# A hybrid attention and delta-rule layer on one core: blocks of the transposed probabilities moved inside SBUF, two more units for the heads, another slab order

## Chip, core and metric

One core of a Trainium2 chip runs one layer in float32. The metric is the time of one execution in microseconds on the device (us); before and after are compared by the medians of several runs. The profile is of one execution of its own, taken by the hardware profiler.

## What is computed

x is 512 x 1024. After an RMS norm, one wide projection gives the inputs of two branches, and of their gates:

```python
q = apply_rope(rms_norm(heads(aq, 8, 128), q_norm), cos, sin)      # attention: 8 heads
k = apply_rope(rms_norm(heads(ak, 2, 128), k_norm), cos, sin)      # 2 kv heads
v = heads(av, 2, 128)
s = einsum('qd,sd->qs', q_i, k) * 128 ** -0.5                      # per head, 512 x 512
o_att = softmax(s) @ v
y_att = (o_att * silu(az)) @ w_br_att
o_dn = bidir_gated_deltanet(...)                                   # delta rule, both directions
y_dn = (rms_norm(o_dn) * silu(dz)) @ w_br_dn
mix = (sigmoid(gate_att) * y_att + sigmoid(gate_dn) * y_dn) @ w_out
x = x + rms_norm(mix, norm_post)
x = x + rms_norm(sigmoid(x @ w_ple_gate) * (p @ w_ple_proj), ple_norm)
```

The change concerns the step from softmax(s) to its product with v, and the order in which the projections' weights come.

## The kernel before

**Matmuls.** A float32 product is made of three matmuls on halves that add up to the operand: lo x hi, hi x lo and hi x hi. `split` (L250) makes them: a cast on ACT gives hi, and a subtraction on DVE or on POOL gives lo, whichever the planner holds to be done first. Weights come as slabs of 512 KB (128 x 1024): `fetch` (L487) loads a slab into one of two buffers `wraw`, `loader` (L502) splits it into one of two pairs `whi`, `wlo`, and `gemm_t` (L532) runs 24 matmuls of 512 columns on it. Weights of the matrices kv, q0, q1, out0, out1, pg0 and pg1 come as four blocks of the same size each, and for out0 to pg1 are split into units instead of the pair. Fetching and loading go strictly in the order of `names`, which is ORDER with the blocks set in; OUT0 names the four slabs ahead of which the blocks of out0 stand.

**The planner.** The Python code is a discrete simulation. Each part of the work (a generator) waits for buffers and events in planned time, and each instruction is given to an engine with a planned duration. The order so found is what each engine gets; on the chip each engine runs its list in order and waits by semaphores. ORDER gives the sequence of the large products on TensorE, PR the priority of the other parts, and EXPS, EOUT, COOL and HOT are thresholds of its choices.

**DMAs.** All transfers are issued from SyncE (SP) by `Q` (L216), except two at the very end from ACT. The built program has eight semaphores for transfers (DMAHW0 to 7), taken in turn: a transfer can be issued only when the one that had its semaphore before has landed.

**Units.** SBUF holds 17 large units u0 to u16 of 8 KB per partition, given from one use to the next. u0 to u3 hold the normed input until the last projection from it (`free_h`), u9 and u10 the queries of heads 0 to 3. HEADU names the units for the heads.

**A head** (`att_head`, L1525). For each of four tiles of 128 queries: three matmuls for the scores (L1539 to 1541), maximum on DVE, exponential and row sum on ACT, and a transpose of 32 x 32 blocks on DVE into the unit T. The blocks still have to be moved across partitions: each tile is written to DRAM (P<-u), four transfers of 256 KB per head, and read back into a second unit L by four more (u<-P). The reciprocal row sums go to DRAM as one row (SR<-rrow) and come back spread over all partitions (c<-SR); POOL multiplies them into the head's gate (gi<-gi,c). For each of four blocks of keys, L is then split (cast on ACT, subtraction on POOL or DVE into `blk`) and three matmuls add to the product with v (L1576 to 1578). Between the heads' steps TensorE runs the output projection of the delta branch (ydn), and after the last head that of the attention branch (yatt), then out0, out1, pg0 and pg1. Each head needs two units, and three are named in HEADU.

Of the kernel before, what the change touches and what calls it, by code (L numbers as in the profile page):

```python
# [35 lines left out]
class Flow:  # L36
# [40 lines left out]
    def op(self, eng, dur, dep, fn, *a, **k):  # L77

        engs = eng if isinstance(eng, tuple) else (eng,)
        t, at = self.slot(engs, dur, dep)
        for e, i in zip(engs, at):
            self.eng[e].insert(i, (t, t + dur))
        if fn is not None:
            self.n += 1
            if eng == "POOL" and dur >= LONG:
                fn = self.behind(t, fn)
            elif engs[1:] == ("POOL",):  # L90
                fn = self.shutting(t + dur, fn)
            heapq.heappush(self.later, (t, self.n, fn, a, k))
        return t + dur
# [69 lines left out]


ORDER = """
dk3 dk2 dq0 dq2 dq3 dq1 dk0 dk1 dz3 dv2 dq5 dk4 dv3 dv0 dq7 dz6
dz7 dq6 gB2 dk7 gA3 gA0 dk5 gB6 gA5 dz1 az3 dv1 dq4 az4 dk6 dz2
az0 gA7 gA6 dz0 az5 az2 dv4 dv6 dv7 gA1 gB4 gB1 gB5 az7 dz4 dv5
kv az6 gA2 gB0 gA4 q0 dz5 gB7 q1 gB3 az1 free_h ydn0 ydn1 ydn2 ydn5
ydn4 ydn7 ydn3 ydn6 yatt6 yatt3 yatt0 yatt7 yatt5 yatt2 yatt1 vec yatt4 out0 out1 pg0  # L170
pg1
"""
OUT0 = 'yatt2 ydn6 ydn3 yatt0'
PR = dict(dec=6, dm1=2, y=4, conv=2, gate=3, kv=4, q=8, head=0, ple=8, prep=8, tab=7)
GAP = 0.0
EXPS = 1.11
SPARE = ((15, "raw", 7.0, 190.0), (11, "pair", 22.0, 80.0), (12, "pair", 22.0, 80.0), (14, "pair", 279.0, 375.0))
EOUT = 34.23
WIDE = 2.0
LAND = "c2"  # L180
LONG, NEAR = 0.6, 1.5
X_DVE = ()
WARM = 5.5
W1 = 0
COOL, HOT = 2.23, 1.12
HEADU = ("u13", "u14", "u16")


@with_exitstack
def layer(ctx, tc, x, xT, pw0, wp1, wt, wba, wn, rows, qkn, hd16, npost, pnorm, dnorm, cs, out):  # L190
# [22 lines left out]
    def G(dur, dep, fn, *a, **k):  # L213
        return op("POOL", dur, dep, fn, *a, **k)

    def Q(kb, dep, o, i, by=sync):  # L216

        t = op("DGE" if by is sync else "ACT", 0.46, dep, by.dma_start, o, i)
        return op("DMA", kb * 0.31, t + 0.5, None) + 1.3

    sb = ctx.enter_context(tc.tile_pool(name="sb", bufs=1))
# [18 lines left out]
    def dram(name, shape):  # L240
        return dr.tile(shape, F32, name=name, tag=name)
# [82 lines left out]
    load, ple, late = {}, {}, {}  # L324
# [177 lines left out]
    def loader(names):  # L502
        for name in names:
            yield "ev", fetched[name]
            raw, t = load[name]
            if name[:2] in places:
                us, j = places[name[:2]], name[2]
                his, los = blocks.setdefault(name[1], ([], []))
                if name[1] == "out0" and j >= 2:
                    yield "ev", landed  # L510
                if j % 2 == 0:
                    for u, lst in ((us[j // 2], his), (us[j // 2 + 2], los)):
                        yield "get", f"u{u}"
# [12 lines left out]
            yield "at", t - 0.3  # L526
            _, tl = split(raw, hi, lo, t, 1024, True, soon=name is names[0])
            free(held["raw", name], tl)
            slab[name][0].set(tl + 0.2)
            slab[name][1] = (hi, lo)  # L530
# [985 lines left out]

    head_ev = {}
    att_start = Event()
    SR = dram("SR", [8, 32, 4, 32])
    rinv = const([128, 32], "rinv")  # L1520
    rrow = [const([128, 32], f"rrow{i}") for i in range(2)]
# [3 lines left out]
    def att_head(h):  # L1525
        hb, kv, b = h % 4, h // 4, h // 4
        qh, ql = qbs[b]
        akT, av = akv["k"], akv["v"]
        yield "any", HEADU
        uT = int(F.got[1:])  # L1530
        T = unit(uT, [128, 4, 4, 4, 32])
        B = dram(f"P{h}", [4, 32, 4, 512])
        for t in range(NT):
            cc = slice(t * 128, (t + 1) * 128)
            yield "get", "c2"
            P = tile("c2", [128, 512])
            yield "get", "aux"
            sc = bank("aux")
            pe.matmul(sc, ql[:, hb, cc], akT[:, 0, kv, :], start=True, stop=False)  # L1539
            pe.matmul(sc, qh[:, hb, cc], akT[:, 1, kv, :], start=False, stop=False)  # L1540
            pe.matmul(sc, qh[:, hb, cc], akT[:, 0, kv, :], start=False, stop=True)
            yield "pe", 0.682
            mx, bi, li = (sm[:, t, i, h:h + 1] for i in range(3))
            ri = rinv[:, 4 * h + t:4 * h + t + 1]
            rs = saq[:, t, h:h + 1]
            te = V(0.62, 0.0, dve.reduce_max, mx, sc, axis=AX.X)
            te = V(0.15, te, dve.tensor_scalar, out=bi, in0=mx, scalar1=rs, scalar2=-1.0, op0=ALU.mult, op1=ALU.mult)
            te = A(0.68, te, act.activation, P, sc, AF.Exp, bias=bi, scale=rs, accum_out=li)
            free("aux", te)
            tr = V(0.15, te, dve.reciprocal, ri, li)  # L1550
            te = V(0.64, te, dve.transpose, T[:, :, t].rearrange("p a j q -> p j a q"), P)
            free("c2", te)
            tw = Q(2, te, B[:, :, :, t * 128:(t + 1) * 128].rearrange("P i a n -> (P i) a n"),
                   T[:, :, t].rearrange("p a j q -> p a (j q)"))
        free(f"u{uT}", tw)
        tr = V(0.15, tr, dve.transpose, rrow[h % 2], rinv)
        tr = Q(0.2, tr, SR[h].rearrange("t P i -> P t i"), rrow[h % 2])
        yield "at", tw - 1.0
        yield "any", HEADU
        uL = int(F.got[1:])  # L1560
        L = unit(uL, [128, 4, 4, 4, 32])
        for a in range(4):
            tl = Q(2, tw, L[32 * a:32 * a + 32].rearrange("p P t j q -> p P (t j q)"), B[:, :, a, :].rearrange("P i n -> i P n"))
        uz, tz = yield from gate_in("az", h)
        yield "get", "c2"
        rb = tile("c2", [128, 512])
        tr = Q(2, tr, rb, row(SR[h, 4 * h:4 * h + 4].rearrange("t P i -> (t P i)"), 512))
        tz = G(1.19, max(tz, tr), pool.tensor_mul, uz, uz, rb)
        free("c2", tz)
        yield "at", tl - 0.3  # L1570
        yield "get", "aux"
        po = bank("aux")
        dd_ = slice(kv * 128, kv * 128 + 128)

        def pv(kt, pT):
            pe.matmul(po, av[:, 1, kt, dd_], pT[:, 0], start=(kt == 0), stop=False)  # L1576
            pe.matmul(po, av[:, 0, kt, dd_], pT[:, 1], start=False, stop=False)
            pe.matmul(po, av[:, 0, kt, dd_], pT[:, 0], start=False, stop=(kt == NT - 1))
            free("blk", F.now + 0.7)

        pend = []
        for kt in range(NT + 1):
            if kt < NT:
                yield "get", "blk"
                pT = tile("blk", [128, 2, 512], F32R)
                src = L[:, :, :, kt, :].rearrange("p P t q -> p t P q")
                hi, lo = (pT[:, i].rearrange("p (t P q) -> p t P q", t=4, P=4) for i in range(2))
                pend.append((kt, pT, split(src, hi, lo, tl, 512, True)[1]))
            if kt > 0:
                k_, p_, t_ = pend.pop(0)  # L1590
                yield "at", t_ + 0.3
                pv(k_, p_)
                yield "pe", 0.682
        free(f"u{uL}", t_)
        if turn("landed") == 7:
            landed.set(F.now)
        if ya[b] is None:
            us = ((0, 1), (2, 3))[b]
            ya[b] = "pending"
            for u in us:  # L1600
                yield "get", f"u{u}"
            ya[b] = tuple(unit(u, [128, 4, 512], F32R) for u in us)
        while ya[b] == "pending":
            yield "at", F.now + 1.0
        t = V(0.66, tz, dve.tensor_mul, po, po, uz)
        free("gi", t)
        _, t = split(po, ya[b][0][:, hb, :], ya[b][1][:, hb, :], t, 512)
        free("aux", t)
        if turn(("head", b)) == 3:
            for u in ((9, 10), (11, 12))[b]:  # L1610
                free(f"u{u}")
        if turn("head") == 7:
            for u in (6, 15):
                free(f"u{u}")
        return t + 0.2
# [398 lines left out]
```

## Time and profile before

| | |
|---|---|
| Median of three runs | 765.58 us (764.84 to 766.57) |
| The profiled execution: time | 763.64 us |
| The profiled execution: span, first to last instruction | 761.9 us |
| Mean granted TensorE clock | 0.986 |
| Instructions | 11858 |
| Moved by DMA | 130.01 MB, 171 GB/s over the span |
| HBM read, written | 97.60 MB, 31.62 MB |

The profile names an instruction by line, engine, operation and tiles (out<-in, buffer numbers left out). All operations that the planner places have the lines of its helpers (L124, L97, L102), so they are told apart by their tiles. PE is TensorE's matmul, PEld its weight load; matmuls overlap, so a busy PE is not PE at its peak. A granted clock under 1.00 means that TensorE was throttled.

### The profile page before, as it was taken

What the parts mean: (1) busy time and instruction counts of PE and PEld (TensorE: products, weight loads), DVE (VectorE), ACT (ScalarE), POOL (GpSimd) and SP (SyncE); (2) the same over time, 40 slices, a digit from 0 to 9 for tenths busy, and PEclk for the clock granted to TensorE, in tenths of its full rate; (3) what the DMA queues carried; (4) which work ended last, traced back from release to release, by engine and by line L of the source; (5) the groups of instructions that cost most, each with busy time, mean ns of one, the idle gap of its engine ahead of it and who ended that gap; (6) DMA issues with size and microseconds to landing.
All of it is one profiled execution on the core that took longest, in us unless ns stands there. A gap on an engine that the chain in (4) does not pass through costs nothing.

```text
span 761.9 us, 11858 instructions
## 1 busy us (share of the span) xinstructions
PE 731.4 (96%) x4313; PEld 607.8 (80%) x4313; DVE 475.0 (62%) x928; ACT 359.8 (47%) x704; POOL 339.8 (45%) x291
## 2 busy tenths in 40 slices
PE   9999999999999999999999999999788889999995
PEld 7787888888789988888898888878666657888885
DVE  4588889897865568997755428687464324313334
ACT  6669464765643263444432354555454333242422
POOL 5837575211542253203411355385476575562511
PEclk9999999999999999999999999999898999999998
DMA  8684547764711227557211325859978956753313
GB/s 344 214 270 152 156 151 213 262 223 151 208 44 42 88 94 202 194 196 201 67 42 43 111 97 166 251 147 251 286 205 256 275 201 223 236 161 126 97 64 117
DMA packets 89707, 130.01 MB, mean 171 GB/s; under 512 B 24560, under 2 KB 50096, under 8 KB 89648
## 3 DMA queue, kind: packets, MB, share of 16 engines
q1 hardware_dynamic: 89360, 128.99, 53.3%
q8 instruction: 34, 0.56, 0.3%
q10 hardware_dynamic: 288, 0.26, 0.1%
q14 instruction: 25, 0.20, 0.1%
HBM read 97.60 MB, written 31.62 MB: 170 GB/s over the span
## 4 chain that ended last, share of the span: by engine, by line
PE 74%; DMA 11%; DVE 4%; POOL 3%; SPq 2%; ACT 2%; issue 2%; POOLq 0%; DVEq 0%; ACTq 0%
PE mm L543 13%; PE mm L545 13%; PE mm L544 13%; PE mm L562 4%; PE mm L564 4%; PE mm L563 4%; DMA wraw<-in_wt_dram 3%; PE mm L580 3%; PE mm L581 3%; PE mm L582 3%; DMA P<-u 2%; DMA u<-P 2%; PE aux L1212 2%; PE aux L1244 2%; SPq L124 2%
## 5 line engine op out<-in xcount | busy, mean ns | idle before, releaser
L543 PE MATMUL mm<-u,wlo 128*128 128x512 f32 x520 | 209.8, 403 | 3.7 <-POOL wlo L102 1.9
L102 POOL TENSOR_TENSOR wlo<-wraw,whi 128x1024 fp32r<-128x1024 f32 x53 | 127.1, 2398 | 179.3 <-ACT whi L124 156.4
L544 PE MATMUL mm<-u,whi 128*128 128x512 f32 x520 | 203.7, 392 | 0.2 <-DVE u L124 0.2
L545 PE MATMUL mm<-u,whi 128*128 128x512 f32 x520 | 203.9, 392 | 0.0
L543 PEld LDWEIGHTS mm<-u,wlo 128*128 128x128 f32 x520 | 98.3, 189 | 25.7 <-POOL wlo L102 3.9
L545 PEld LDWEIGHTS mm<-u,whi 128*128 128x128 f32 x520 | 98.2, 189 | 21.1
L544 PEld LDWEIGHTS mm<-u,whi 128*128 128x128 f32 x520 | 98.4, 189 | 18.9 <-DVE u L124 0.5
L124 ACT CAST whi<-wraw 128x1024 fp32r<-128x1024 f32 x65 | 68.1, 1049 | 79.0 <-PE mm L545 41.5
L124 DVE SCALAR_TENSOR_TENSOR f<-mm,cw,f 128x510 f32<-128x510 f32 (+1 forms) x96 | 71.5, 746 | 10.0 <-ACT f L124 7.5
L124 DVE TENSOR_TENSOR u<-aux,u 128x512 f32<-128x512 f32 (+2 forms) x60 | 39.3, 668 | 24.0 <-ACT u L124 16.4
L562 PE MATMUL mm<-u,u 128*128 128x512 f32 (+1 forms) x136 | 52.0, 382 | 0.0
L102 POOL TENSOR_TENSOR u<-wraw,u 128x1024 fp32r<-128x1024 f32 x18 | 43.1, 2402 | 19.4 <-ACT u L124 19.2
L564 PE MATMUL mm<-u,u 128*128 128x512 f32 (+1 forms) x136 | 51.3, 377 | 0.0
L563 PE MATMUL mm<-u,u 128*128 128x512 f32 (+1 forms) x136 | 51.2, 377 | 0.0
L102 POOL TENSOR_TENSOR blk<-u,blk 128x512 fp32r<-128x512 f32 x32 | 40.4, 1283 | 1.3 <-ACT blk L124 1.1
L124 ACT ACTIVATE c<-aux,sm,saq 128x512 f32<-128x512 f32 x32 | 24.9, 778 | 30.5 <-DVE sm L124 29.0
L124 ACT COPY c<-aux 128x512 f32<-128x512 f32 x18 | 10.6, 586 | 51.6 <-DVE f L124 26.8
L580 PE MATMUL mm<-whi,u 128*128 128x512 f32 x88 | 34.8, 395 | 0.0
L581 PE MATMUL mm<-wlo,u 128*128 128x512 f32 x88 | 34.4, 391 | 0.0
L582 PE MATMUL mm<-whi,u 128*128 128x512 f32 x88 | 34.4, 390 | 0.0
L124 ACT CAST u<-aux 128x512 fp32r<-128x512 f32 (+1 forms) x28 | 15.4, 555 | 38.2 <-PE aux L1749 13.8
L973 ACT ACTIVATE u<-u,cj 128x64 f32<-128x64 f32 x104 | 26.2, 336 | 7.4 <-POOL u L102 7.4
(257 smaller groups left out, 1402.6 us busy)
## 6 DMA issues: line engine op xcount, KB each, us to landing
wraw<-in_wt_dram SPq DMA_DIRECT2D x58, 512.0 KB, 3.9
wraw<-in_wn_dram SPq DMA_DIRECT2D x28, 512.0 KB, 4.1
P<-u SPq DMA_DIRECT2D x32, 256.0 KB, 5.3
u<-P SPq DMA_DIRECT2D x32, 256.0 KB, 5.7
u<-in_wt_dram SPq DMA_DIRECT2D x14, 512.0 KB, 5.9
u<-CI SPq DMA_DIRECT2D x16, 256.0 KB, 4.1
u<-in_x_dram SPq DMA_DIRECT2D x4, 512.0 KB, 8.4
u<-in_xT_dram SPq DMA_DIRECT2D x4, 512.0 KB, 8.2
```

Source lines behind the costliest of these rows:

```text
L102: ins = fn(*a, **k)
L124: fn(*a, **k)
L543: pe.matmul(o, lo[:, k, :], mh(k), start=(k == 0), stop=False)
L544: pe.matmul(o, hi[:, k, :], ml(k), start=False, stop=False)
L545: pe.matmul(o, hi[:, k, :], mh(k), start=False, stop=(k == 7))
L562: pe.matmul(o, b, hi, start=(i == 0), stop=False)
L563: pe.matmul(o, a, lo, start=False, stop=False)
L564: pe.matmul(o, a, hi, start=False, stop=(i == 7))
L580: pe.matmul(o[t], b, hi, start=(k == 0), stop=False)
L581: pe.matmul(o[t], a, lo, start=False, stop=False)
L582: pe.matmul(o[t], a, hi, start=False, stop=(k == 7))
L973: act.activation(e, e, AF.Exp, bias=cj[:, d, c, 4 * g + h, i:i + 1])
```

## The change

- The write to DRAM and the read back are replaced by 16 transfers inside SBUF per head. Transfer i takes the 32 partitions of block row P = i mod 4 at a = i div 4, and puts them at the 32 partitions of block row a; each is 64 KB, in runs of 2 KB. The pieces with i mod 4 = 2 are issued from ACT (XACT), four of 16, the others from SyncE. All of them need all four tiles of the head.
- HEADU has five units for each half of the heads: u2 and u3 for heads 0 to 3, u9 and u10 for heads 4 to 7, beside the three of before.
- A head from the fourth on starts only when the head three before it has got its unit L (GATE, `land_ev`).
- All four blocks of out0, not only the last two, wait for the event that the last head's L has been split (`landed`).
- ORDER, OUT0, PR, EXPS, EOUT, COOL and HOT have new values.

```diff
 ORDER = """
-dk3 dk2 dq0 dq2 dq3 dq1 dk0 dk1 dz3 dv2 dq5 dk4 dv3 dv0 dq7 dz6
+dk3 dk0 dk1 dq0 dq1 dq3 dk2 dv2 dz4 dq2 dq5 dk6 dk5 gB3 dv1 dq6
...
-OUT0 = 'yatt2 ydn6 ydn3 yatt0'
-PR = dict(dec=6, dm1=2, y=4, conv=2, gate=3, kv=4, q=8, head=0, ple=8, prep=8, tab=7)
+OUT0 = 'yatt1 yatt3 yatt6 yatt0'
+PR = dict(dec=2, dm1=4, y=8, conv=7, gate=0, kv=7, q=4, head=1, ple=5, prep=8, tab=9)
...
-EXPS = 1.11
+EXPS = 1.04
...
-EOUT = 34.23
+EOUT = 25.06
...
-COOL, HOT = 2.23, 1.12
-HEADU = ("u13", "u14", "u16")
+COOL, HOT = 1.24, -1.15
+XACT = (2,)
+GATE = 3
+HEADU = (("u13", "u14", "u16", "u2", "u3"), ("u13", "u14", "u16", "u9", "u10"))
...
-                if name[1] == "out0" and j >= 2:
+                if name[1] == "out0":
                     yield "ev", landed
...
-        yield "any", HEADU
+        if h >= GATE:
+            yield "ev", land_ev[h - GATE]
+        yield "any", HEADU[b]
         uT = int(F.got[1:])
         T = unit(uT, [128, 4, 4, 4, 32])
-        B = dram(f"P{h}", [4, 32, 4, 512])
...
-            tw = Q(2, te, B[:, :, :, t * 128:(t + 1) * 128].rearrange("P i a n -> (P i) a n"),
-                   T[:, :, t].rearrange("p a j q -> p a (j q)"))
-        free(f"u{uT}", tw)
...
-        yield "at", tw - 1.0
-        yield "any", HEADU
+        yield "at", te - 0.5
+        yield "any", HEADU[b]
         uL = int(F.got[1:])
+        land_ev[h].set(F.now)
         L = unit(uL, [128, 4, 4, 4, 32])
-        for a in range(4):
-            tl = Q(2, tw, L[32 * a:32 * a + 32].rearrange("p P t j q -> p P (t j q)"), B[:, :, a, :].rearrange("P i n -> i P n"))
+        for i in range(16):
+            a, P = divmod(i, 4)
+            tl = Q(0.5, te, L[r32(a), P].rearrange("p t j q -> p (t j q)"), T[r32(P), a].rearrange("p t j q -> p (t j q)"),
+                   act if i % 4 in XACT else sync, 0.38)
+        free(f"u{uT}", tl)
```

**SyncE, one of the middle heads.** Before: the last writes of one head stand among the first of the next, and reads, gate and row sums come between (P is the copy in DRAM, u a unit, c the tile for the row sums, wraw a slab):

```order
L124 DMA P_5383<-u_742_5382 512x1x128 x2
L124 DMA go_5477<-gate_gB 128x512
L124 DMA mixB<-go_5355 128x512
L124 DMA P_5383<-u_742_5382 512x1x128
L124 DMA SR<-rrow_118 4x32x32
L124 DMA u_772_5539<-P_5383 32x4x512
L124 DMA P_5507<-u_767_5506 512x1x128
L124 DMA u_772_5539<-P_5383 32x4x512 x3
L124 DMA gi_5540<-gate_az 128x512
L124 DMA c_774_5541<-SR 128x512
```

After, the same place:

```order
L124 DMA wraw_5540<-in_wt_dram 128x1024
L124 DMA SR<-rrow_118 4x32x32
L124 DMA go_5604<-gate_gB 128x512
L124 DMA mixB<-go_5478 128x512
L124 DMA u_779_5630<-u_746_5448 32x512 x12
L124 DMA gi_5631<-gate_az 128x512
L124 DMA c_781_5632<-SR 128x512
```

Twelve transfers from unit to unit have taken the place of four writes and four reads, in one run; the gate and the row sums still come behind them.

**ACT, the first head.** Before, with the semaphores that an instruction waits for, from the last exponential to the first casts of L (blk):

```order
L124 ACTIVATE c_661_4922,sm<-aux_4923,sm,saq 128x512 [waits DVE_49,Activation_49]
L124 CAST whi_4948<-wraw_4850 128x1024 [waits DMAHW6_49,PE_49,Pool_49]
L124 CAST blk_4962<-u_657_4892 128x512 [waits DMAHW2_49,DMAHW7_49,DMAHW1_49,DMAHW0_49]
L124 CAST blk_4963<-u_657_4892 128x512
L124 CAST whi_4993<-wraw_4903 128x1024 [waits DMAHW7_49,PE_49,Pool_49]
```

After, from the four issues to the first cast:

```order
L124 DMA u_648_4881<-u_629_4768 32x512 [waits DVE_49,PE_49]
L124 DMA u_648_4881<-u_629_4768 32x512 [waits DMAHW5_49]
L124 CAST u_573_4429<-mm_4876 128x512 [waits DVE_49]
L124 DMA u_648_4881<-u_629_4768 32x512 [waits DMAHW0_49]
L124 DMA u_648_4881<-u_629_4768 32x512 [waits DMAHW2_49]
L124 CAST whi_4927<-wraw_4862 128x1024 [waits PE_49,Pool_49]
L124 CAST blk_4943<-u_648_4881 128x512 [waits DMAHW4_49,DMAHW5_49,DMAHW3_49,DMAHW6_49,DMAHW2_49,DMAHW7_49,DMAHW1_49,DMAHW0_49]
```

Four issues have come in between exponentials and casts; three of them wait for an earlier transfer, and the first cast now waits on all eight semaphores.

**POOL, from the last head into yatt.** Before (wlo is a slab's lo half, u<-wraw that of a block of out0):

```order
L102 TENSOR_TENSOR gi_5915<-gi_5915,c_843_5916 128x512
L102 TENSOR_TENSOR blk_5960<-u_841_5914,blk_5960 128x512
L102 TENSOR_TENSOR blk_5961<-u_841_5914,blk_5961 128x512
L102 TENSOR_TENSOR wlo_5983<-wraw_5928,whi_5982 128x1024
L102 TENSOR_TENSOR blk_6002<-u_841_5914,blk_6002 128x512
L102 TENSOR_TENSOR blk_6011<-u_841_5914,blk_6011 128x512
L102 TENSOR_TENSOR u_864_6038<-wraw_5966,u_863_6037 128x1024
L102 TENSOR_TENSOR wlo_6048<-wraw_6020,whi_6047 128x1024
L102 TENSOR_TENSOR wlo_6091<-wraw_6070,whi_6090 128x1024
L102 TENSOR_TENSOR wlo_6130<-wraw_6085,whi_6129 128x1024
L102 TENSOR_TENSOR u_864_6038<-wraw_6124,u_863_6037 128x1024
```

After:

```order
L102 TENSOR_TENSOR blk_6022<-u_833_5946,blk_6022 128x512
L102 TENSOR_TENSOR gi_6006<-gi_6006,c_842_6007 128x512
L102 TENSOR_TENSOR blk_6038<-u_833_5946,blk_6038 128x512
L102 TENSOR_TENSOR wlo_6040<-wraw_5917,whi_6039 128x1024
L102 TENSOR_TENSOR blk_6055<-u_833_5946,blk_6055 128x512
L102 TENSOR_TENSOR blk_6076<-u_833_5946,blk_6076 128x512
L102 TENSOR_TENSOR u_858_6100<-wraw_6015,u_857_6099 128x1024
L102 TENSOR_TENSOR wlo_6110<-wraw_6087,whi_6109 128x1024
L102 TENSOR_TENSOR u_858_6100<-wraw_6130,u_857_6099 128x1024
L102 TENSOR_TENSOR wlo_6160<-wraw_6145,whi_6159 128x1024
L102 TENSOR_TENSOR wlo_6192<-wraw_6186,whi_6191 128x1024
```

The multiplication by the row sums has moved behind the head's first subtraction, and behind the last head two blocks of out0 stand ahead of the next slabs where one stood (the third and fourth follow later in yatt).

More of the change, by code (lines that the diff above doesn't have):

```diff
@@ L165 @@
 ORDER = """
-dk3 dk2 dq0 dq2 dq3 dq1 dk0 dk1 dz3 dv2 dq5 dk4 dv3 dv0 dq7 dz6
[L167 to L170, printed above, removed]
-pg1
-"""
-OUT0 = 'yatt2 ydn6 ydn3 yatt0'
-PR = dict(dec=6, dm1=2, y=4, conv=2, gate=3, kv=4, q=8, head=0, ple=8, prep=8, tab=7)
+dk3 dk0 dk1 dq0 dq1 dq3 dk2 dv2 dz4 dq2 dq5 dk6 dk5 gB3 dv1 dq6
+gB7 az2 dv3 gA0 dz0 az4 gA2 gB4 dz1 gA4 dk4 dv0 dz7 dq7 dk7 dq4
+dz6 az7 gB5 az3 dz3 dz2 dv6 dv4 dv5 gA3 gB6 gA6 az0 az6 gA5 dv7
+kv az5 gB0 gB2 gA1 q0 dz5 gA7 q1 az1 gB1 free_h ydn1 ydn0 ydn6 ydn2
+ydn5 ydn3 ydn7 ydn4 yatt4 yatt7 yatt6 yatt1 yatt2 yatt0 yatt5 vec yatt3 out0 out1 pg0
+pg1
+"""
+OUT0 = 'yatt1 yatt3 yatt6 yatt0'
+PR = dict(dec=2, dm1=4, y=8, conv=7, gate=0, kv=7, q=4, head=1, ple=5, prep=8, tab=9)
 GAP = 0.0
-EXPS = 1.11
+EXPS = 1.04
 SPARE = ((15, "raw", 7.0, 190.0), (11, "pair", 22.0, 80.0), (12, "pair", 22.0, 80.0), (14, "pair", 279.0, 375.0))
-EOUT = 34.23
+EOUT = 25.06
 WIDE = 2.0
@@ L214, in G, with Q @@
         return op("POOL", dur, dep, fn, *a, **k)
-    def Q(kb, dep, o, i, by=sync):
-        t = op("DGE" if by is sync else "ACT", 0.46, dep, by.dma_start, o, i)
+    def Q(kb, dep, o, i, by=sync, dur=0.46):
+        t = op("DGE" if by is sync else "ACT", dur, dep, by.dma_start, o, i)
         return op("DMA", kb * 0.31, t + 0.5, None) + 1.3
@@ L1518, in layer @@
     att_start = Event()
+    land_ev = [Event() for _ in range(8)]
     SR = dram("SR", [8, 32, 4, 32])
```

## The prediction

> **What bounds the kernel now.** I read the page's busy times first: TensorE has work almost all the time.
>
> ```profile
> PE 731.4 (96%) x4313; PEld 607.8 (80%) x4313; DVE 475.0 (62%) x928; ACT 359.8 (47%) x704; POOL 339.8 (45%) x291
> ```
>
> The change leaves the number of matmuls alone, so all it can win is TensorE's idle time and its slow clock. The windows by 20 us say where these lie (per engine: busy us and instructions; then granted clock, DMA share, GB/s).
>
> ```profile
> 320.00:340.00 20.00, 20.00 (x90) 16.57 (x89) 18.85 (x45) 8.23 (x15) 0.00 (x0) 1.00 0.63 217
> ...
> 520.00:540.00 20.00, 16.94 (x73) 13.34 (x71) 11.57 (x27) 9.18 (x19) 12.51 (x9) 0.97 1.02 285
> 540.00:560.00 20.00, 17.86 (x69) 14.24 (x69) 13.26 (x32) 10.65 (x22) 13.42 (x10) 0.86 0.79 222
> 560.00:580.00 20.00, 17.40 (x69) 13.42 (x67) 10.66 (x25) 8.96 (x19) 10.93 (x7) 0.91 0.88 244
> 580.00:600.00 20.00, 14.39 (x55) 11.22 (x55) 9.52 (x21) 10.74 (x20) 12.47 (x10) 0.91 0.93 297
> 600.00:620.00 20.00, 17.99 (x70) 13.42 (x68) 2.77 (x4) 4.94 (x8) 15.61 (x10) 0.91 0.74 225
> 620.00:640.00 20.00, 18.29 (x80) 14.75 (x79) 8.10 (x12) 7.54 (x9) 11.89 (x5) 1.00 0.56 182
> 640.00:660.00 20.00, 18.45 (x81) 14.95 (x81) 7.41 (x12) 6.39 (x8) 9.59 (x5) 1.00 0.63 210
> ```
>
> A full window holds 90 matmuls of 512 columns. From 520 to 620 us, where the attention heads run, TensorE is idle for 3.06 + 2.14 + 2.60 + 5.61 + 2.01 = 15.4 us, and the missing clock (0.03 + 0.14 + 0.09 + 0.09 + 0.09) x 20 costs another 8.8 us: **24.2 us lost**. From 620 to 660, in the output projection of the attention branch (yatt), 1.71 + 1.55 = 3.3 us more are idle. Nothing else that the change reaches is as large.
>
> Why the heads are slow: the timeline of SyncE's queue has one transfer SR<-rrow per head.
>
> ```profile
> 520.23 0.55 SPq L124 DMA_DIRECT2D SR<-rrow  x1
> ...
> 597.37 0.57 SPq L124 DMA_DIRECT2D SR<-rrow  x1
> ```
>
> These are the first and last of six, so 77.1 / 5 = 15.4 us per head. Of 15.4 us TensorE needs only 15.4 x (1 - 24.2 / 100) = 11.7. In the windows 520 to 600 POOL is busy for 49.33 us (9.5 per head), DVE for 45.01 (8.7), ACT for 39.53 (7.6): none of them fills 15.4 by its work. The list of waits gives POOL a second part, and tells what TensorE waits for (total us, times, longest).
>
> ```profile
> POOL gi L102 <- DMA c<-SR: 35.7, 7, 8.8
> ...
> PE aux L1577 <- POOL blk L102: 12.3, 9, 3.1
> PE aux L1576 <- ACT c L124: 3.1, 1, 3.1
> ```
>
> POOL waits 35.7 / 7 = 5.1 us per head, in order, for the broadcast of the row sums, and its subtractions for the probabilities (blk) stand behind that: 9.5 + 5.1 = 14.6 of the 15.4 us. The broadcast is issued behind the head's reads of P, and those behind its writes. These transfers (KB, median us to landing) are late because the DMA share there is 0.74 to 1.02.
>
> ```profile
> P<-u SPq DMA_DIRECT2D x32, 256.0 KB, 5.3
> u<-P SPq DMA_DIRECT2D x32, 256.0 KB, 5.7
> ...
> c<-Bdk SPq DMA_DIRECT2D x32, 64.0 KB, 2.1
> ...
> c<-SR SPq DMA_DIRECT2D x8, 256.0 KB, 6.6
> ...
> go<-mixB SPq DMA_DIRECT2D x8, 256.0 KB, 3.7
> ...
> dB<-u SPq DMA_DIRECT2D x8, 64.0 KB, 3.2
> ```
>
> **The change, part by part.**
>
> The transposed probabilities. Issue times on SyncE (min/median/max, ns), and on ACT in the fourth row:
>
> ```profile
> L124 SPq DMA_DIRECT2D P<-u x32: 513/519/976, 472.7 to 596.8; - x32
> L124 SPq DMA_DIRECT2D u<-P x32: 318/432/1052, 482.2 to 602.7; - x32
> L124 SPq DMA_DIRECT2D c<-Bdk x32: 318/427/492, 49.3 to 222.0; - x32
> L124 ACTq DMA_DIRECT2D out_dram<-wlo x2: 338/357/376, 757.7 to 758.4; - x2
> ```
>
> Now, from the last transposed tile to the landed head: 0.52 + 5.3 (write) + 4 x 0.43 + 5.7 (read) = 13.2 us. After: twelve issues on SyncE, 12 x 0.43 = 5.1, and the last piece lands 2.1 later: **7.2 us**. No row shows an SBUF to SBUF transfer. The nearest are c<-Bdk (64 KB into 32 partitions, 2.1) and dB<-u (64 KB out of 32 partitions, 3.2). With 3.2, and the second eight pieces queued behind the first, it is at most 5.1 + 2 x 3.2 = 11.5. I take 2.1, because the runs of each piece are 2 KB, against 128 B in dB; the range keeps 11.5. Either way 8.4 MB of writes and 8.4 MB of reads (32 x 256 KB each) become one move of 8.4 MB, so all other transfers get room.
>
> SyncE's price: 12 x 0.43 instead of 4 x 0.52 + 4 x 0.43, so 1.3 us more per head. Queued behind the twelve are the head's gate, the broadcast c<-SR, mixB and the next weights: six issues of at most 0.57, 3.4 us, which with 5.1 makes 8.5 of 11.7. That cover is gone if a wait inside the twelve exceeds 3 us. ACT's four issues cost 4 x 0.36 = 1.4 us, and an in-order wait for the landing of an earlier piece, of 0 to 3.2, holds exponentials and casts behind it: 7.6 + 1.4 + 2.1 = 11.1 us, just under TensorE's 11.7.
>
> On coalescing: the row is 2.1 us for 64 KB, against 5.3 for 256 KB. The Trainium skill ("DMA: Bandwidth & Descriptors", Rules for kernel authors) says that many small transfers should be made one, and that under 64 KB one pays mostly overhead. By that rule the sixteen pieces are the wrong direction, and their fixed cost returns as the rival "in series" below.
>
> Units and the gate. A head holds one unit for the tile that it writes and one for the tile that it reads back. Three units let one head fill while another drains; five let two more stand between. GATE holds a head back until the head three before it has its landing unit, which stops nothing that five units could feed. I price both at nothing: TensorE's 11.7 us per head is the cover, and without it the units give back the pace of now.
>
> What is late next: POOL's wait for c<-SR. It is now issued behind the twelve: 5.1 + 2 x 0.43 = 6.0 us after the last tile. It lands at 9.7 by the row of go<-mixB (3.7, a stage with DMA room) or 12.6 by its own row (6.6). POOL reaches it, behind one subtraction, at 7.2 + 0.6 (cast) + 1.28 = 9.1:
>
> ```profile
> L102 POOL TENSOR_TENSOR blk<-u,blk 128x512 fp32r<-128x512 f32 x32 | 40.4, 1283 | 1.3 <-ACT blk L124 1.1
> L102 POOL TENSOR_TENSOR u<-wraw,u 128x1024 fp32r<-128x1024 f32 x18 | 43.1, 2402 | 19.4 <-ACT u L124 19.2
> ```
>
> POOL then waits 0.6 to 3.5 us, and has 10.1 to 13.0 us per head. I take a wait of 2.5, nearer the broadcast's own row, so 12.0 against TensorE's 11.7. Over 100 / 15.4 = 6.5 heads that leaves 0.3 x 6.5 = 2.0 us idle, and 1 us for the last head, which nothing follows: 3.0 (0 to 1.3 x 6.5 = 8.5).
>
> The clock. Behind short waits the chain shows matmuls at 0.43 us instead of 0.23:
>
> ```profile
> 569.61 0.43 PE mm L543
> ...
> 586.72 0.23 PE aux L1540
> ```
>
> So 15.4 us of idle time brought 8.8 of slow clock, a factor of 1.57: 3.0 become **4.7 us** (0 to 13.3). The Trainium skill ("TensorE: Matmul & The Clock Gate", Why this matters for your kernels) puts the loss of clock at idle gaps over about 3 us. By that rule gaps this short would cost no clock and the term would be 3.0; here the longest recorded wait is 3.1 us and four slices stand at 0.86 to 0.91, so the trace decides.
>
> The weights of out0. All four blocks now wait for the last head, where two did, and the new list puts them between the yatt slabs; before, two stood between the ydn slabs. The loader works in order, so a slab behind a block waits for its load, cast and subtraction. The chain has one such place:
>
> ```profile
> 635.29 2.43 POOL wlo L102
> 637.74 5.11 DMA wraw<-in_wt_dram
> 642.95 1.06 ACT whi L124
> 644.08 2.38 POOL wlo L102
> 646.50 0.50 PE mm L543
> ```
>
> TensorE lost up to 1.6 us in that window. Two more such places cost 2 x 1.6 = 3.2; with the P traffic over, loads are shorter, so I take **+2** (-1 to +6).
>
> The rest (slab order, priorities, split thresholds) moves the same instructions. TensorE's idle time outside heads, yatt and the last 22 us is small (PE busy in the first column):
>
> ```profile
> 0.00:20.00 20.00, 18.02 (x81) 14.62 (x81) 10.33 (x16) 13.33 (x23) 10.91 (x38) 1.00 0.88 340
> ...
> 200.00:220.00 20.00, 19.24 (x388) 15.33 (x388) 17.80 (x27) 9.14 (x17) 10.59 (x6) 1.00 0.24 82
> ```
>
> These two largest losses are 1.98 and 0.76 us. The new order may lose or keep as much again: 0 (-2 to +3).
>
> **The sum.** -24.2 + 4.7 + 2 + 0 = -17.5 us, against the profiled execution: span 761.9 us, time 763.64, so 746.1. The median of the runs shown is 765.58, 1.94 above it: **748 us**.
>
> **The rivals.**
>
> - POOL stays the pace. If c<-SR still takes 6.6 us, POOL has 13.0 per head: 8.5 us idle, 13.3 with the clock: -24.2 + 13.3 + 2 = -8.9, 757 us. For it: its row, and 14.6 of 15.4 now. Against it: the DMA room that the change makes. Chance 0.16.
> - In series (the slower side). If the pieces don't overlap, a head occupies the queues for 16 x 2.1 = 33.6 us, 18 more than the pace of now: over 6.5 heads +118 us, 884 us. It decides from 15.4 / 16 = 0.96 us per piece; at 1.2 us, 19.2 per head, it is already +25, 790 us. For it: each piece spans 32 partitions, and only eight can be under way. Against it: four c<-Bdk of 64 KB are issued 0.43 apart and still land in 2.1. The Trainium skill ("SBUF — State Buffer", The DMA setup-cost knee) gives every transfer a fixed cost of about 2 us, which a loop of 64 KB tiles pays again and again; by the trace, issues overlap it. Chance 0.08.
> - The loader becomes the bound. If a slab behind each of the four blocks waits for a whole load, cast and subtraction (5.1 + 1.1 + 2.4 = 8.6) where a slab's 24 matmuls cover 5.3, that is 4 x 3.3 = 13.2 instead of 3.3, with the clock 15.5 more: -24.2 + 4.7 + 15.5 = -4, 762 us. Chance 0.06.
> - It changes nothing. The heads gain in landing, but ACT's waits for pieces (to 3.2 instead of 2.1, and a slab's landing on top) hold the exponentials so long that the pace stays near 15: within 1.5 us of 765.6. Chance 0.04.
>
> **How the numbers follow.** The forecast has the remaining 0.66; its own range, with most of each term's bounds, is -27 to -10: 738 to 756. Taking in the POOL rival and part of the loader's, the range is 738 to 760; what it leaves out is slower (0.08), no change (0.04) and the ends, under 0.2 together. A measurement of this kernel (764.84 to 766.57 in three runs) tells about 0.2%, 1.5 us, from no change. Faster: 0.66 + 0.16 + 0.06 = 0.88; same 0.04; slower 0.08.
>
> **What would show it.** Right: pieces issued 0.4 to 0.5 us apart and landing in 2 to 3.5; SR<-rrow every 11.7 to 13 us; windows of the heads at 19 us busy or more, with the clock at 0.97 or more; HBM writes down by 8.4 MB; DMA share under 0.7 in the heads. Wrong: pieces landing after more than 5 us, POOL waiting over 3.5 us per head for c<-SR, ACT idle ahead of its DMA issues for over 3 us, or over 6 us idle in yatt.

## The result, and the profile after

The changed kernel takes **789.29 us** (median of four runs, 786.59 to 789.66). The kernel before takes 765.74 (median of four, 764.84 to 766.57). The ratio is 1.030, with a 95% interval of 1.0274 to 1.0326: slower by 23.6 us, where 17.5 us less was forecast. The profiled execution took 789.1 us with a span of 787.4, so 25.5 us more span than before.

In the page of the changed kernel, TensorE has the same 4313 matmuls and is busy for 7 us more, at a mean granted clock of 0.977 for 0.986. As forecast, 8.4 MB less is written to HBM. The DMA rows give size and median time to landing. The chain of work that ended last is summed by engine in the last two rows, where SPq is SyncE's queue.

```profile
PE 738.6 (94%) x4313; PEld 610.3 (78%) x4313; DVE 470.8 (60%) x924; ACT 363.0 (46%) x724; POOL 344.1 (44%) x293
...
HBM read 89.21 MB, written 23.23 MB: 143 GB/s over the span
## 4 chain that ended last, share of the span: by engine, by line
PE 76%; DMA 8%; SPq 6%; POOL 4%; DVE 2%; issue 2%; ACT 2%; POOLq 0%; DVEq 0%; ACTq 0%
...
u<-u SPq DMA_DIRECT2D x96, 64.0 KB, 2.0
...
u<-u ACTq DMA_DIRECT2D x32, 64.0 KB, 3.4
...
c<-SR SPq DMA_DIRECT2D x8, 256.0 KB, 4.2
```

The same row of the chain for the kernel before, which the prediction had not looked at:

```profile
PE 74%; DMA 11%; DVE 4%; POOL 3%; SPq 2%; ACT 2%; issue 2%; POOLq 0%; DVEq 0%; ACTq 0%
```

The transfers did get shorter: the pieces land in 2.0 us on SyncE, and the broadcast of the row sums in 4.2 instead of 6.6. DMA's share of the chain fell from 11% to 8%. But the share of SyncE's queue, the time in which the chain waits for SyncE to get round to an issue, rose from 2% (15 us) to 6% (47 us).

The windows of the changed kernel, to be set beside those of before (PE's busy time in the second column, granted clock and DMA share third and second from the end):

```profile
480.00:500.00 20.00, 15.82 (x70) 12.59 (x69) 7.83 (x19) 7.48 (x15) 8.86 (x6) 0.98 0.53 159
500.00:520.00 20.00, 20.00 (x88) 16.37 (x87) 15.12 (x31) 7.76 (x13) 13.72 (x17) 0.93 0.41 113
520.00:540.00 20.00, 17.74 (x76) 13.25 (x75) 12.82 (x33) 11.27 (x24) 11.06 (x7) 1.00 0.55 153
540.00:560.00 20.00, 16.31 (x69) 13.04 (x68) 11.01 (x28) 9.65 (x19) 8.44 (x5) 0.91 0.59 161
560.00:580.00 20.00, 15.81 (x60) 12.44 (x59) 10.59 (x24) 7.12 (x14) 9.81 (x7) 0.83 0.50 157
580.00:600.00 20.00, 15.57 (x67) 11.96 (x65) 9.00 (x25) 8.82 (x18) 8.60 (x6) 1.00 0.67 171
600.00:620.00 20.00, 14.54 (x48) 10.57 (x48) 7.19 (x16) 8.31 (x15) 13.48 (x10) 0.83 0.69 190
620.00:640.00 20.00, 13.95 (x54) 9.39 (x52) 3.80 (x6) 5.13 (x9) 12.25 (x9) 0.98 0.55 170
640.00:660.00 20.00, 19.73 (x81) 15.81 (x81) 7.35 (x12) 7.26 (x9) 13.24 (x6) 0.93 0.58 189
660.00:680.00 20.00, 17.15 (x64) 13.54 (x63) 5.28 (x8) 6.15 (x8) 9.21 (x5) 0.83 0.76 235
680.00:700.00 20.00, 19.88 (x88) 16.16 (x87) 5.57 (x8) 6.69 (x11) 12.07 (x8) 1.00 0.47 153
700.00:720.00 20.00, 18.62 (x85) 15.20 (x84) 5.61 (x5) 5.58 (x11) 10.96 (x9) 1.00 0.62 215
```

From 480 to 640 us TensorE is idle for 4.18 + 2.26 + 3.69 + 4.19 + 4.43 + 5.46 + 6.05 = 30.3 us and loses 0.54 x 20 = 10.8 by the clock: 41 us. In the kernel before these windows lost 17.4 (the 15.4 of the prediction, 0.28 in the one from 480 and 1.71 in the one from 620) and 8.8: 26. So 15 of the 25.5 us are lost in the heads, with DMA less busy than before in every slice that the prediction shows for that stretch up to 640. Most of the rest is lost behind them: from 640 to 720 the idle time is 0.27 + 2.85 + 0.12 + 1.38 = 4.6 us and the clock 0.24 x 20 = 4.8, together 9.4, against 1.6 before.

The timeline of SyncE's queue shows one head of the changed kernel, from one SR<-rrow to the next (start, duration, transfer, how many in a run):

```profile
582.56 0.59 SPq L124 DMA_DIRECT2D SR<-rrow  x1
583.25 0.41 SPq L124 DMA_DIRECT2D wraw<-in_wt_dram  x1
583.82 11.19 SPq L124 DMA_DIRECT2D u<-u  x12
595.05 0.58 SPq L124 DMA_DIRECT2D gi<-gate_az  x1
595.73 0.40 SPq L124 DMA_DIRECT2D mixB<-go  x1
596.18 0.43 SPq L124 DMA_DIRECT2D go<-gate_gB  x1
596.71 0.45 SPq L124 DMA_DIRECT2D c<-SR  x1
597.25 0.58 SPq L124 DMA_DIRECT2D SR<-rrow  x1
```

SyncE needs 14.7 us for one head, 11.2 of them for twelve pieces. By its list of waits (582 to 598 us), 3.8 us of this are waits for an earlier transfer to land: 2.3 for a piece, 1.5 for SR<-rrow. The broadcast c<-SR is issued 1.7 us after the run of pieces and 14.1 us after the SR<-rrow that it reads. How long a run takes varies; the shortest of the eight:

```profile
507.26 7.67 SPq L124 DMA_DIRECT2D u<-u  x12
```

That is 0.64 us per piece where nothing else is in the way. Over the eight heads the runs take 8.00 + 7.67 + 8.11 + 10.33 + 8.45 + 11.19 + 9.36 + 11.51 = 74.6 us, 9.3 per head. At 0.64 us the 96 issues would take 61.4, so some 13 us are such waits or longer issues. The row of the issues, and the waits of the other engines for what stands behind them:

```profile
L124 SPq DMA_DIRECT2D u<-u x96: 507/589/1379, 483.2 to 623.3; - x96
```

```profile
POOL gi L102 <- DMA c<-SR: 45.1, 7, 12.8
...
PE aux L1582 <- POOL blk L102: 20.7, 10, 4.8
```

POOL waits 45.1 / 7 = 6.4 us per head for the broadcast (5.1 before), and TensorE 20.7 us for POOL (12.3 before). In six of the eight heads the product of gate and row sums (gi) stands in POOL's order ahead of all the head's subtractions (blk), so these wait with it. Only the second head and the last, whose order stands ahead of the prediction, have one subtraction in front. In those two POOL waits 2.0 and 2.4 us ahead of the product, in the other six 4.0 to 12.8. The second head and the third:

```profile
525.98 1.29 POOL L102 TENSOR_TENSOR gi<-gi,c 128x512 f32<-128x512 f32 x1 [1.95 <-DMA c<-SR]
...
547.38 1.26 POOL L102 TENSOR_TENSOR gi<-gi,c 128x512 f32<-128x512 f32 x1 [12.81 <-DMA c<-SR]
```

From the first SR<-rrow (481.2) to the eighth (611.3) it is 18.6 us per head, 16.8 before.

### The profile page after: what moved, and what is told of

Same layout as the page of the kernel before. It is cut to its first block, busy times and chain, and to the rows that moved or that the text cites. A ratio compares the mean times of both kernels' runs of the same rounds, so it can differ in the third digit from the quotient of the medians.

```text
span 787.4 us, 11948 instructions
## 1 busy us (share of the span) xinstructions
PE 738.6 (94%) x4313; PEld 610.3 (78%) x4313; DVE 470.8 (60%) x924; ACT 363.0 (46%) x724; POOL 344.1 (44%) x293
## 4 chain that ended last, share of the span: by engine, by line
PE 76%; DMA 8%; SPq 6%; POOL 4%; DVE 2%; issue 2%; ACT 2%; POOLq 0%; DVEq 0%; ACTq 0%
PE mm L545 14%; PE mm L546 14%; PE mm L547 14%; SPq L124 6%; PE mm L566 3%; PE mm L564 3%; PE mm L565 3%; PE mm L582 2%; PE mm L583 2%; PE mm L584 2%; DMA wraw<-in_wt_dram 2%; PE aux L1214 2%; POOL wlo L102 2%; PE aux L1246 2%; DMA c<-SR 2%
## 5 line engine op out<-in xcount | busy, mean ns | idle before, releaser
L102 POOL TENSOR_TENSOR wlo<-wraw,whi 128x1024 fp32r<-128x1024 f32 x55 | 131.6, 2393 | 177.6 <-ACT whi L124 149.9
L124 DVE SCALAR_TENSOR_TENSOR f<-mm,cw,f 128x510 f32<-128x510 f32 (+1 forms) x96 | 71.5, 745 | 14.4 <-ACT f L124 11.8
L102 POOL TENSOR_TENSOR u<-wraw,u 128x1024 fp32r<-128x1024 f32 x19 | 45.4, 2395 | 24.8 <-ACT u L124 24.7
L1582 PE MATMUL aux<-blk,u 128*128 128x512 f32 x32 | 15.4, 481 | 20.7 <-POOL blk L102 20.7
L124 ACT COPY c<-aux 128x512 f32<-128x512 f32 x18 | 10.5, 586 | 50.7 <-PE aux L1214 25.5
L975 ACT ACTIVATE u<-u,cj 128x64 f32<-128x64 f32 x120 | 30.0, 335 | 7.1 <-POOL u L102 7.1
```

The lines of the kernel that those rows point to most:

```text
L102: ins = fn(*a, **k)
L124: fn(*a, **k)
L975: act.activation(e, e, AF.Exp, bias=cj[:, d, c, 4 * g + h, i:i + 1])
```

## The experiments

The theory after the result, A: each piece costs SyncE 0.6 us or more to issue, whatever it moves, and what stands in order behind the twelve comes late. Rivals: B, the new tables of order and thresholds make the loss. C, the landing of the probabilities themselves is late. D, ACT's four issues hold exponentials and casts. E, only eight transfers can be under way. Each experiment was run beside the kernel before; the ratio is to it, with a 95% interval. The medians of the kernel before lie between 765.57 and 766.08 in all of them, so times of different experiments are set beside one another.

**Old tables.** ORDER, OUT0, PR, EXPS, EOUT, COOL and HOT, and the condition on out0's blocks, as before; pieces, units and gate as after:

```diff
-EXPS = 1.04
+EXPS = 1.11
...
-                if name[1] == "out0":
+                if name[1] == "out0" and j >= 2:
```

> The sixteen pieces, the five units and the gate, with everything else as before: slab order, priorities, split thresholds, places of out0's weights. Theory A (the pieces hold SyncE's queue; the loss is theirs): 780 to 795 us, pieces again 8 us or more per head on SyncE. Rival B (the new tables make the loss): at or under 766 us. A mixture of the two would fall between.

Measured: 786.04 us, ratio 1.0279 (1.0246 to 1.0312), beside 1.030 for the whole change, and in A's range. The loss is there without the tables.

**Old moves.** The changed kernel with the way over DRAM:

```diff
-        for i in range(16):
...
+        for a in range(4):
+            tl = Q(2, tw, L[32 * a:32 * a + 32].rearrange("p P t j q -> p P (t j q)"), B[:, :, a, :].rearrange("P i n -> i P n"))
```

> The changed kernel with the way over DRAM put back (four writes and four reads per head); new tables, five units and gate stay. Theory A: 758 to 770 us, near the kernel before. Rival B (tables): 782 or more.

Measured: 765.51 us, ratio 0.9997 (0.9973 to 1.0021). With the first run this settles B: the pieces make the loss, and tables, two more units and gate together make no difference that can be told.

**Early sums.** The loads of gate and row sums stand ahead of the pieces in the program:

```diff
+        uz, tz = yield from gate_in("az", h)
+        yield "get", "c2"
+        rb = tile("c2", [128, 512])
+        tr = Q(2, tr, rb, row(SR[h, 4 * h:4 * h + 4].rearrange("t P i -> (t P i)"), 512))
         for i in range(16):
```

> The changed kernel with the gate's load and the broadcast of the row sums (c<-SR) put into the program ahead of the sixteen pieces. Theory A, in the form that POOL is held by c<-SR behind the pieces: POOL's wait for c<-SR falls from 45 us to under 20, and the time to 766 to 780. Rival C (it is the landing of the probabilities themselves that is late, the broadcast only happens to come last): 785 to 795 us, POOL's wait turns into waits for the pieces.

Measured: 770.96 us, ratio 1.0083 (1.005 to 1.0116). Of 23.6 us, 18 are gone with the same sixteen pieces. POOL's waits ahead of the product fell from 50.7 us (45.1, and 5.6 put down to the pieces) to 26.5 (11.6, 10.9 put down to the pieces, 4.0 to VectorE), TensorE's wait for POOL from 20.7 to 4.9, and ACT's casts now wait for the pieces (12.3 us in the changed kernel):

```profile
ACT blk L124 <- DMA u<-u: 32.9, 8, 6.7
...
POOL gi L102 <- DMA c<-SR: 11.6, 4, 4.7
POOL gi L102 <- DMA u<-u: 10.9, 3, 5.3
...
PE aux L1582 <- POOL blk L102: 4.9, 6, 1.3
```

**All on SyncE.** `XACT = ()` instead of `(2,)`.

> All sixteen pieces on SyncE, none on ACT. Theory A: four more issues of some 0.8 us per head on the queue that is the pace, 3.2 us x 6.5 heads = 21 us and clock on top: 805 to 825. Rival D (ACT's four issues and their waits hold exponentials and casts, and make the loss): 770 to 785. Rival E (only eight transfers can be under way, whichever engine issues them): 786 to 792.

Measured: 797.72 us, ratio 1.0426 (1.0391 to 1.0461). Four more issues per head on SyncE cost 8 us: against D, whose relief of ACT does not show, and against E as the whole (its part are the waits for earlier transfers, some 13 us of the changed kernel's eight runs at most), but under A's range. Whether moving the four off ACT gave something back, or part of them was hidden, was not separated.

**Late product.** POOL's product that waits for the broadcast goes behind the head's subtractions:

```diff
-        tz = G(1.19, max(tz, tr), pool.tensor_mul, uz, uz, rb)
-        free("c2", tz)
...
         free(f"u{uL}", t_)
+        tz = G(1.19, max(tz, tr), pool.tensor_mul, uz, uz, rb)
+        free("c2", tz)
```

> The changed kernel with one POOL instruction moved: the product of gate and row sums (gi), which waits for c<-SR, is placed behind the head's subtractions instead of ahead of them. The sixteen pieces and all DMAs stay as they are. Theory A1 (the pieces cost time because POOL, in order, waits for the broadcast that is issued behind them): POOL's wait for c<-SR under 15 us in sum, time 766 to 778, about what the earlier broadcast gave. Rival C (the landing of the probabilities, and so the length of SyncE's queue itself, is the pace): 782 to 792.

Measured: 774.91 us, ratio 1.0132 (1.0098 to 1.0165). The edit touches no transfer (the planner puts some of SyncE's in another order), and 14 us are gone, more than half of the loss. POOL's wait for c<-SR is gone from the list; VectorE, which uses the product at the end of a head, waits 19.3 us for it instead, and TensorE's wait for POOL falls from 20.7 us to:

```profile
PE aux L1580 <- POOL blk L102: 5.7, 10, 1.1
```

**Late product, kernel before.** The same edit of the kernel before.

> The kernel before with the same POOL instruction moved behind the subtractions. Theory A1: the same wait (35.7 us in seven heads) paced the heads of the kernel before, so 748 to 760. Rival F (in the kernel before the bytes over DRAM pace the heads, the wait only lies beside it): 764 to 768.

Measured: 762.70 us, ratio 0.9979 (0.9957 to 1.0001), between the two ranges and nearer to F's. In that kernel the same wait was worth 3 us at most. POOL no longer waits for c<-SR, but for ACT's casts (1.1 us before, from 468 to 660 us), and those for the reads over DRAM (11.8 us before):

```profile
POOL blk L102 <- ACT blk L124: 28.5, 6, 7.1
...
ACT blk L124 <- DMA u<-P: 23.6, 7, 6.7
```

All that TensorE waits for from 468 to 660 us adds up to 18.3 us, for 19.0 in the kernel before. This falls on the prediction's account of the kernel before: POOL's wait for c<-SR was long, but not what paced the heads.

**Half on ACT.** Early sums with `XACT = (0, 2)`, eight pieces on each engine.

> The kernel of the earlier broadcast (770.96 us), with eight of the sixteen pieces on ACT instead of four. Theory A: SyncE loses four issues of 0.6 to 0.8 us per head, 2.4 to 3.2 us: 755 to 768 us. Rival D (ACT is held by issues and their waits, which delays exponentials and casts): 773 to 790.

Measured: 777.32 us, ratio 1.0163 (1.0119 to 1.0206), 6 us worse than with four on ACT. So D is half right: four pieces on ACT do less harm than on SyncE, eight do more. Pieces in ACT's queue also wait, and exponentials behind them:

```profile
ACT c L124 <- DMA u<-u: 23.8, 4, 6.7
...
PE aux L1543 <- ACT c L124: 13.0, 6, 3.2
```

The Trainium skill ("DMA: Bandwidth & Descriptors", Rules for kernel authors) says that spreading transfers over the issuing engines brings no bandwidth and only saves the issuer's time. These runs agree as to the issuer's time (797.7 us with none on ACT, 789.3 with four), and add that the engine which takes the issues over pays for them (771.0 with four, 777.3 with eight); bandwidth was not measured.

**Double.** Every piece in two, 32 of 32 KB per head, same bytes:

```diff
+            for s in (slice(0, 2), slice(2, 4)):
+                tl = Q(0.25, te, L[r32(a), P, s].rearrange("p t j q -> p (t j q)"), T[r32(P), a, s].rearrange("p t j q -> p (t j q)"),
```

> The changed kernel with every piece cut in two: 32 transfers of 32 KB per head, 24 on SyncE, same bytes. If the price is one per issue (0.59 us each): 12 x 0.59 = 7.1 us more per head, over eight heads 57 us and clock on top: 840 to 880. If the price follows the bytes, or the landing of what is under way: 785 to 800, and the issues fall towards 0.3 us.

Measured: 837.43 us, ratio 1.0948 (1.0917 to 1.0979), 48 us above the changed kernel. The issues and the first run of 24:

```profile
L124 SPq DMA_DIRECT2D u<-u x192: 507/589/1198, 485.2 to 677.9; - x192
```

```profile
485.24 16.07 SPq L124 DMA_DIRECT2D u<-u  x24
```

The median issue is 589 ns for 32 KB as for 64 KB, and 24 take 16.07 us (0.67 each) where 12 took 7.67 to 11.5. The price is one per issue. At 837 us the range of 840 to 880 was missed by 3 us; "by the bytes", 785 to 800, is out. By the rule of the Trainium skill ("DMA: Bandwidth & Descriptors", Rules for kernel authors) that small transfers should be made one, which the prediction weighed, this is the direction that loses. The runs agree: 837.4 us with 32 pieces per head, 789.3 with 16.

**No moves, and unread pieces.** Both leave out the exchange of blocks between partitions, so their results are not the layer's. In the first, L is T itself; in the second the pieces are issued as in the changed kernel, into a unit that nothing reads, and the products read T:

```diff
-        L = unit(uL, [128, 4, 4, 4, 32])
+        uL, L, tl = uT, T, te
```

```diff
-                src = L[:, :, :, kt, :].rearrange("p P t q -> p t P q")
+                src = T[:, :, :, kt, :].rearrange("p P t q -> p t P q")
```

> The changed kernel without the sixteen pieces: the products with V read the tile as the 32x32 transposes left it (left out: the exchange of 32-row blocks between partitions). All else, the row sums' way over DRAM too, stays. It shows the most that any cheaper transfer could bring. If the prediction's 24 us of loss in the heads hung on the transfer: 738 to 752 us. Theory G (a head's other steps and the end of the heads, which nothing follows, cost most of it): 754 to 764.

> As the last, but the sixteen pieces are issued and land in a unit that nothing reads, so nobody waits for their landing; SyncE's queue is as long as in the changed kernel. Theory A1 (the issues, 7.7 to 11.5 us per head ahead of the broadcast and the gate, are the cost): 778 to 792. Rival C (the landing of the probabilities is the cost): within 6 us of the kernel without pieces.

Measured: 749.56 us (0.978; 0.9757 to 0.9803) and 778.82 us (1.0151; 1.0122 to 1.0181). From 749.6, issuing the pieces leads to 778.8 (+29), and waiting for their landing and using the data to 789.3 (+10.5). The 29 us contain what comes with an issue: ACT's four, the traffic, the second unit and the planner's new order. The wait for c<-SR is back as soon as the pieces are issued, though nobody reads them (unread pieces; then no moves):

```profile
POOL gi L102 <- DMA c<-SR: 40.2, 8, 10.3
```

```profile
POOL gi L102 <- DMA c<-SR: 9.6, 6, 2.9
```

And the chain of the kernel without moves, by engine:

```profile
PE 87%; DVE 4%; POOL 3%; issue 2%; ACT 2%; DMA 2%; POOLq 0%; DVEq 0%; ACTq 0%; SPq 0%
```

SyncE's queue (6% in the changed kernel) has gone from the chain, and DMA is down from 8% to 2%. From 480 to 640 us this kernel loses 4.8 us of idle time and 3.6 of clock, together 8.4, where the kernel before loses 26 and the changed one 41.

**Four pieces by VectorE.** Early sums, with the pieces whose source and target partitions agree copied on VectorE, 9 issues on SyncE and 3 on ACT:

```diff
+            if a == P:
+                tl = max(tl, V(0.6, te, dve.tensor_copy, L[r32(a), P].rearrange("p t j q -> p (t j q)"), T[r32(P), a].rearrange("p t j q -> p (t j q)")))
+                continue
```

> The kernel of the earlier broadcast (770.96 us), in which the four pieces that stay on their own partitions are copied by VectorE (four of 32x512 per head) instead of transferred: 9 issues on SyncE and 3 on ACT. Theory A: SyncE saves 3 x 0.6 to 0.8 and ACT one issue, about 2 us per head: 755 to 766. Rival H (VectorE, with four copies of about 0.6 us more per head, becomes the pace): 770 to 785.

Measured: 771.90 us, ratio 1.0096 (1.0059 to 1.0134), as early sums alone and in H's range. No gain shows from what SyncE saved; VectorE has four copies of 0.8 us per head to make:

```profile
L124 DVE COPY u<-u 32x512 f32<-32x512 f32 x32 | 25.6, 799 | 0.4
```

**The planner told 0.7 us.** In the changed kernel, 0.7 instead of 0.38 as the duration of a piece's issue, by which the planner lays out the order of all engines:

```diff
-                   act if i % 4 in XACT else sync, 0.38)
+                   act if i % 4 in XACT else sync, 0.7)
```

> The changed kernel, with the planner told 0.7 us per piece's issue instead of 0.38, so that the order of all engines is laid out for the length that SyncE's run has. If the order written for too short an issue makes the loss: 765 to 776. If the length itself does: 782 to 792.

Measured: 780.33 us, ratio 1.0183 (1.0163 to 1.0204). Between the two ranges: with this order 9 us less are lost. That they came of an order laid out for issues shorter than they are is not shown, for the next run has the same figure and is slower.

**Both remedies.** Early sums and 0.7 us.

> The changed kernel with both remedies: the broadcast of the row sums ahead of the pieces, and the planner told 0.7 us per issue. If the two act on different losses: 789.3 less 18 less 9, 760 to 766. If they are two remedies for the same loss (things late behind SyncE's run): 766 to 774, like the better one alone.

Measured: 796.25 us, ratio 1.0408 (1.0371 to 1.0444). Both expectations missed: together the remedies are worse than nothing. The timeline of SyncE shows the last two heads behind one another:

```profile
606.74 0.42 SPq L124 DMA_DIRECT2D go<-mixB  x1
613.13 0.32 SPq L124 DMA_DIRECT2D gi<-gate_az  x1
613.50 0.42 SPq L124 DMA_DIRECT2D c<-SR  x1
613.98 8.33 SPq L124 DMA_DIRECT2D u<-u  x12
631.61 0.33 SPq L124 DMA_DIRECT2D gi<-gate_az  x1
632.04 0.38 SPq L124 DMA_DIRECT2D c<-SR  x1
632.47 8.23 SPq L124 DMA_DIRECT2D u<-u  x12
```

SyncE stands still ahead of both loads of the gate. Its list of waits for 570 to 645 us has:

```profile
SPq L124 <- DVE aux L124: 15.1, 2, 9.2
```

The gate has two buffers, which VectorE's product at the end of an earlier head sets free. In this order the load stands ahead of the pieces and waits for it, so the pieces of a head wait for the end of another. That is read from the trace and was not tried by itself. It also bounds how far the differences above may be trusted: here a new order costs 25 us (796.3 against 771.0 of early sums alone) for a reason of its own, so a difference of that size shows a cause only where the waits in the trace go with it.

**The kernel before, with less waiting.** Broadcast ahead of the reads of P and the product behind the subtractions; then the way over DRAM with the new tables, five units, gate and the late product:

> The kernel before, way over DRAM, with the broadcast c<-SR issued ahead of the reads of P and the product of gate and row sums behind the subtractions. If POOL's wait for the broadcast paces the heads there as the prediction said: 750 to 758. If the bytes over DRAM and a head's chain of steps do: 760 to 766.

> Way over DRAM with the new tables, five units and the gate, and the product of gate and row sums behind the subtractions. If the units pay once POOL is free of its wait: 750 to 759. If the way over DRAM paces: 760 to 766.

Measured: 766.63 us (1.0009; 0.9985 to 1.0033) and 760.88 us (0.9958; 0.9935 to 0.9982). The first is 0.6 us above both of its ranges and says again that POOL's wait did not pace the heads of the kernel before. The second lies in the range for the way over DRAM as the pace, and beats both kernels, by 0.4% against the one before. What does pace the heads over DRAM is left open: in that last kernel casts wait for the reads (27.0 us in seven waits), and the DMA share is 0.90 to 1.02 from 520 to 600 us.

```profile
ACT blk L124 <- DMA u<-P: 27.0, 7, 8.9
```

## Why the prediction was wrong, point by point

- **SyncE's price, the step that failed.** "12 x 0.43" took an issue from the rows of u<-P and c<-Bdk. Measured: 0.589 the median, 0.64 from one to the next, so 7.7 us per head without waits and 9.3 with them, for 5.1. The prediction's own fences had dearer rows: P<-u at 519 ns, and SR<-rrow at 0.55 to 0.57. With 0.57 the run is 6.8 us. That these read SBUF does not tell them from the cheap ones: gate_az<-go and mixB<-go read SBUF too, at 326 and 354 ns in the kernel before. "That cover is gone if a wait inside the twelve exceeds 3 us" named the point: the two longest runs hold 3.5 and 3.8 us of waits (11.19 and 11.51 less 12 x 0.64), and SyncE's work for the head shown takes 14.7 us, where 8.5 of 11.7 was reckoned.
- **POOL's wait for c<-SR.** Taken as 2.5 us of a range of 0.6 to 3.5; measured 6.4 per head. Two steps make it. The broadcast was to be issued 6.0 us after the last tile and to land at 9.7 to 12.6; it is issued 8.7 to 14.4 us after the run of pieces begins, and POOL's product starts 13.7 to 18.7 after it. That follows from the step above. And POOL was to reach the product "behind one subtraction", at 9.1: this was the order of the last head, and six of eight heads have none in front, so POOL stands there earlier and its subtractions stand with it. Early sums (18 us back) and the late product (14 back) show that this is the way by which most of the loss comes; in the unread pieces it comes though nobody waits for their landing.
- **The 24 us of loss in the heads.** The sum left 4.7 of them. That the loss hangs on the transfer was right: with no transfer at all the kernel takes 749.6 us, 16.5 less than before. But then the forecast of 748 was that of a transfer which costs nothing. And the reason given for the loss, POOL's wait, was worth 3 us or nothing in the kernel before. A long wait of a busy engine was taken for the pace without looking at what TensorE's own waits would do when it went.
- **Landing.** Right: 2.0 us on SyncE (2.1 taken), 3.4 on ACT. HBM writes are down by 8.4 MB, and the DMA share in the heads is 0.41 to 0.69. The broadcast, too, lands sooner (4.2 us for 6.6), but it is issued later. Landing and use are 10.5 us of the whole, issuing 29.
- **ACT.** That ACT stays "just under TensorE's 11.7" held for four pieces: TensorE waits 2.9 us for ACT's exponentials (468 to 660 us), and without them on ACT the kernel is 8 us slower. Eight cost 6 us, and that wait is 13.0. Issuing from a third engine was not tried.
- **Units and gate at nothing; out0 +2; the rest 0.** Not contradicted: together with the tables they give 0.9997 (0.9973 to 1.0021) over DRAM, so 0 within 2 us. With the pieces the order matters more (9 us less with 0.7 told to the planner, 25 us more when early sums are told it). The losses from 640 us on (9.4 for 1.6) were not taken apart.
- **The clock.** 10.8 us for 30.3 idle, a factor of 1.36 for 1.57: near enough.
- **The rivals.** "In series" gave 790 us at 1.2 us per piece, with a chance of 0.08. The number came out, but not the way: the pieces overlap in landing, and it is their issues that are in series, at 0.78 us (74.6 / 96), under the 0.96 from which that rival decides; the hit is luck. "POOL stays the pace" (757 us) named the engine that waits and why TensorE waits, not the queue that makes it late. The rival that was missing is the issuing queue itself; the other forecasts all lie below the result. Of the signs of being wrong, POOL's wait over 3.5 us came true (6.4), pieces landing after more than 5 us did not (2.0 and 3.4 at the median).

## What to carry to other kernels

Count the issues of an in-order queue before the bytes: add up, for one period of the loop, every issue on it at the dearest price among the near rows, and ask what stands behind the longest run and who waits for that in order. Before a wait is called the pace, look whether the engine that sets the end waits any less without it; moving one instruction is a cheap test. A kernel that leaves the disputed step out altogether shows about the most that any version of it can bring.

## What the runs showed of the hardware

- The issue of a piece had the same price at two sizes: the median on SyncE is 589 ns at 64 KB and at 32 KB, the least 507 in both. What makes it dearer than the 0.36 to 0.43 us of the issues by which the prediction priced it was not tried. The price of one and the same transfer is not fixed either: the median issue of c<-SR is 404 ns in the kernel before, 446 in the changed one and 319 without pieces.
- Transfers of 64 KB from SBUF to SBUF overlap: issued 0.64 us apart they land in 2.0 us, and those of 32 KB in 1.8. It is the queue and not the move that runs in series.
- VectorE copies 32 x 512 fp32 in 799 ns, and its transposes take 703 ns for 32 x 512 and 694 for 128 x 512 in the same run: a quarter of the partitions was not cheaper.

```profile
L124 DVE STREAM_TRANSPOSE u<-c 32x512 f32<-32x512 f32 x8 | 5.6, 703 | 0.2
```
